# Seven-product output projection: order of the weight loads, order of the second pair's splits, and where two more chunks get their offset

## The chip, the cores and the metric

The kernel runs on one core of a Trainium2 chip. The metric is the device time of one execution in microseconds (us), lower is better. A run of the kernel before was timed three times: 1286.32, 1286.92 and 1287.92 us.

## What is computed

One layer of a bidirectional encoder for 2048 rows of 1024 columns, float32 throughout. A joint input projection feeds a chunked gated linear attention (4 heads) and a latent attention with a softmax (4 heads). Each gives 512 columns. They are joined, go through one output projection, and the residual and a LayerNorm close the layer. The change lies in this last part alone:

```python
def hybrid_mixer(...):
    ...
    return jnp.concatenate([o_a, o_b], axis=-1) @ w_out       # (2048 x 1024) @ (1024 x 1024)

x = layer_norm(DEEPNORM_ALPHA * x + mixed, ln_g, ln_b)        # alpha = 2 ** 0.25
```

## The kernel before, in words

**Products.** TensorE multiplies in a type with a shorter mantissa, so each float32 operand is split into a rounded part (`hi`, line 393, a copy on ScalarE) and a remainder (`lo`, line 400, here a subtraction on GpSimd). `mm3` (line 448) runs three matmuls for one product, so lines 450 to 452 are most of TensorE's work.

**Chunks and pairs.** The output projection works on 16 chunks of 128 rows. Chunks 0 to 7 are multiplied in the plain way: 8 slices of the inner dimension, two halves of 512 columns. They run partly under the last block of the attention, chunks 4 and 5 right behind it, and chunks 6 and 7 at places 0 to 21.76. Chunks 8 to 15 make four pairs (class `Pair`, line 1969). A pair's 256 rows and the 1024 inner columns form 2 x 2 blocks A11, A12 (row 0 of the pair) and A21, A22 (row 1). Instead of eight block products it has seven, P1 to P7, with sums of the blocks (S1 = A21 + A22, S3, S2 = S1 - A11, S4 = A11 - A12, computed in place by `add` on VectorE, line 2016) and with sums of weight blocks. P5, P6 and P7 use the weight combinations wt1, wt2, wt3. P4 uses wt4, which is loaded over the right half (columns 512 on) of the weight tiles 0 to 3, once chunk 7 has read them. The combinations were computed early in the kernel and lie in DRAM as high and low parts: `fetch_t("2l")` loads the low part of wt2, and so on. wt1, wt2 and wt3 have 1 MB a part; the low part of wt3 goes in two loads of 512 KB, into tiles `wt3l` and `wt3m`; wt4 takes eight loads of 256 KB (`fetch_t("4h")`, `"4l"`, line 2213).

**Loads of a pair.** `Pair.load(r)` (lines 1982 to 1995) issues four DMAs of 256 KB for row r of the pair: the first half's data, two gate factors, the second half's data. The gate factors are multiplied in on GpSimd (`gate`, line 2004). The second pair's row 0 goes into a tile that the profile calls `lng`, its row 1 into `lnb`; these are the former tiles of the LayerNorm's scale and offset. All these DMAs are issued by SyncE (SP), in one queue.

**Banks.** The seven products of a pair share four PSUM banks. P1 and P7 use bank 0, P5 and P2 bank 1, P6 bank 2, P3 and P4 bank 3. So P4 may begin when VectorE has read P3 (`R6`), the next pair's P1 when ScalarE has copied P7 (`c7`, line 2041), and its P5 when VectorE has read P2 (`R7`). `read` is lines 2051 and 2053, `sum` line 2044, and the statistics are line 2059.

**Closing a chunk.** `finish_a` subtracts the mean and multiplies by ln_g on VectorE (line 2315; `centre`, line 2084, for row 0). ScalarE makes the reciprocal root (lines 2321 to 2326). `finish_b` multiplies by it and adds ln_b on VectorE (line 2332), once for each half, and issues the stores. Only the last pair's row 0 is closed by ScalarE (scale, line 2094) and GpSimd (offset, line 2095), from a copy of ln_b made by `copy_lnb` (line 2088).

**Order.** Every engine runs its instructions in the order in which they stand. From chunk 6 on, the order is a sort by hand-written places (`put`, and `PLACE_PAIR`, lines 135 to 152); a place is meant as microseconds. Pair p starts at T = 21.76 + 19.05 p. An entry of the second pair with place -9.85 thus stands among the first pair's entries at 9.2. Before chunk 6, the order on ScalarE, GpSimd and SP is that of the code in lines 1907 to 1936.

Of the kernel before, what the change touches and what calls it, by code (L numbers as in the profile page):

```python
# [136 lines left out]
    load1=(-23.6, -35.9),  # L137
    res=(-10.0, -8.0),
    gate=((-19.94, -18.58), (-24.72, -21.3)),
    add=dict(S1=-10.55, S3=-9.85, S2=-8.0, S4=-4.37),  # L140
    hi=dict(A11=-17.26, S1=-9.75, S2=-7.3, A12=-5.39, S3=-4.77, S4=-3.53, A22=-2.66),
    lo=dict(A11=-13.14, S1=-8.45, S2=-6.6, S3=-3.67, A22=1.77, A12=3.13, S4=4.49),
    product=dict(P1=0.0, P5=2.72, P6=5.44, P3=8.16, P7=10.88, P2=13.6, P4=16.32),
    last=dict(P1=0.0, P5=2.72, P6=5.44, P3=8.16, P2=10.88, P7=13.6, P4=16.32),
    gate1=((-14.6, -13.3), (-19.95, -18.6)),
    gate0=((-6.0, -4.7), (-24.72, -21.3)),
    first=dict(hA11=-15.2, hS3=-8.0, hA12=-2.6, lS3=-6.5, lS4=-2.2),
    read=dict(c1=2.78, R1=5.9, R5=6.5, R5b=7.1, U2=9.9, R2=10.5, R6=11.87, c7=14.91, U3=15.63, R3=16.26, bn22=16.89,
              R7=17.52, sq=18.25, R4=20.34, R4b=20.97, bn21=21.6, rs=21.9, fa=(22.9, 22.23), fb=(23.9, 26.7)),
    read_last=dict(c1=2.78, lnb=9.0, R1=3.3, R5=6.3, R5b=6.9, U2=8.9, R2=9.5, R3=10.1, R4b=10.7, R6=11.5, bn12=12.1,  # L150
                   R7=14.1, bn11=14.7, R3p=16.9, R4p=17.5, bn22=18.1, fa=(15.3, 20.2), fb=(17.0, 20.3)),
)

# [232 lines left out]
class K:  # L386
# [1215 lines left out]
    def attention(self):  # L1602
# [4 lines left out]
        with ExitStack() as ctx:  # L1607
# [245 lines left out]
            for k in range(NK):  # L1853
                if k < PRE_W:
                    v = NP * (PRE_BLOCK + k)
                    hi, lo = v + out["pre_hi"], v + out["pre_lo"]
                else:
                    hi = end + out["w_hi"] + (k - PRE_W) * out["w_step"]
                    lo = hi + out["w_lo"]
                if k == 0:  # L1860
                    put(hi - 6, op.fetch_w, k)
                put(hi, op.split_hi, k)
                put(lo, op.split_lo, k)
                if k + 1 < NK:
                    put(lo + 0.01, op.fetch_w, k + 1)
                else:
                    put(max(lo, end + 26) + 0.02, op.load_ln)
                for o, place in zip(first, out["part0"]):
                    put(end + (out["part"][k] if k else place), op.part, o, k)
            for c, o in enumerate(first):  # L1870
# [98 lines left out]
class Pair:  # L1969
# [117 lines left out]
        self.lnb = self.op.bp.tile([P, 2, 512], F32, tag="pl", name="lnbc", bufs=3)  # L2087
        self.nc.scalar.activation(self.lnb, self.op.ln[1], AF.Copy)

    def finish_first(self):  # L2090
        o, c = self.rows[0], self.c[0]
        for n in range(2):
            rr = o["rr"][:, n]
            self.nc.scalar.activation(rr, rr, AF.Copy, scale=o["rs"])
            self.nc.gpsimd.tensor_tensor(rr, rr, self.lnb[:, n], ALU.add)
            self.nc.sync.dma_start(self.k.out[c * P:(c + 1) * P, n * 512:(n + 1) * 512], rr)

    def put(self, put, T, last):
        at = lambda place, fn, *a: put(T + place, fn, *a)
        P_, op = PLACE_PAIR, self.op  # L2100
        first = {} if self.p else P_["first"]
        if self.p:
            for r in (1, 0):
                at(P_["load1" if self.p == 1 else "load"][r], self.load, r)
# [40 lines left out]
        at(e["bn11"], self.stats, 0, 0, 0)  # L2145
        at(e["bn22"], self.stats, 1, 1, 2, 3)
# [6 lines left out]
        at(e["fb"][0], self.finish_first)  # L2153
        at(e["fa"][1], op.finish_a, self.rows[1])
        at(e["fb"][1], op.finish_b, self.rows[1])

# [1 line left out]
class OutProj:  # L2158
# [47 lines left out]
    def fetch_t(self, n):  # L2206


        j, p = int(n[0]), "hl".index(n[1])
        src, kern = self.k.wt_s[j][p], self.k  # L2210
        if j == 4:
            for k in range(4):
                self.nc.sync.dma_start(self.W[k][p][:, 512:].bitcast(F32), src[:, k])
            return
        if n == "3l":
            t = [kern.wof.tile([P, D], F32R, tag="raw", name="wt3l", bufs=1).rearrange("p (a d) -> p a d", a=2),
                 kern.keep.tile([P, 2, QB], F32R, tag="acc", name="wt3m")]
            for i in range(2):
                self.nc.sync.dma_start(t[i].bitcast(F32), src[:, 2 * i:2 * i + 2])
        else:  # L2220
            slot = dict(zip(("1h", "1l", "2h", "2l", "3h"), ("ckvT_h", "ckvT_l", "krs", "vh", "vl")))[n]
            t = kern.rp.tile([P, NKT, P], F32R, tag=f"res_{slot}", name=f"wt{n}").rearrange("p (k a) d -> p k (a d)", k=4)
            self.nc.sync.dma_start(t.bitcast(F32), src)
            t = [t[:, 0:2], t[:, 2:4]]
        self.T[j, p] = t

    def wt(self, j, k):
        return [self.T[j, p][k // 2][:, k % 2] for p in range(2)]
# [64 lines left out]
    def residual(self, o, n):  # L2293
# [6 lines left out]
        nc.vector.bn_stats(o["bn"][:, n], rr)  # L2300

    def finish(self, o):
        self.finish_a(o)
# [98 lines left out]
```

## Time and profile before

| what | value |
|---|---|
| runs shown, median (range) | 1286.92 us (1286.32 to 1287.92) |
| profiled execution, its own time | 1286.29 us |
| its span, first to last instruction | 1284.5 us |
| TensorE busy | 1257.6 us, 98% of the span |
| VectorE / ScalarE / GpSimd busy | 941.5 / 874.0 / 846.9 us |
| mean granted TensorE clock | 0.996 of full speed |

The profile is one execution. Times in its views are microseconds from the span's start; 1.8 us of the execution lie around the span. PE is TensorE, PEld its weight loads, DVE VectorE, ACT ScalarE, POOL GpSimd, SP (or SPq) SyncE, which issues the DMAs. A timeline row has the start, the duration, the engine, the source line, the operation, what is written and read, a count, and in brackets the idle time ahead of it with what ended it. `pw` are the four banks of the pairs, `xr` the rows of a chunk of a pair, `of`, `lng` and `lnb` loaded data of a pair, `A11h` and `A11l` the two parts of a block.

### The profile page before, as it was taken

What the parts mean: (1) busy time and instruction counts of PE and PEld (TensorE: products, weight loads), DVE (VectorE), ACT (ScalarE), POOL (GpSimd) and SP (SyncE); (2) the same over time, 40 slices, a digit from 0 to 9 for tenths busy, and PEclk for the clock granted to TensorE, in tenths of its full rate; (3) what the DMA queues carried; (4) which work ended last, traced back from release to release, by engine and by line L of the source; (5) the groups of instructions that cost most, each with busy time, mean ns of one, the idle gap of its engine ahead of it and who ended that gap; (6) DMA issues with size and microseconds to landing.
All of it is one profiled execution on the core that took longest, in us unless ns stands there. A gap on an engine that the chain in (4) does not pass through costs nothing.

```text
span 1284.5 us, 20176 instructions
## 1 busy us (share of the span) xinstructions
PE 1257.6 (98%) x6928; PEld 1110.4 (86%) x6928; DVE 941.5 (73%) x1706; ACT 874.0 (68%) x1549; POOL 846.9 (66%) x546
## 2 busy tenths in 40 slices
PE   7999999999999999999999999999999999999997
PEld 7999999999889999999788888888888888888785
DVE  6865775656675455555798888888888888658788
ACT  7765657666675656665688888888888888614454
POOL 0244555363667666672188888889999999955762
PEclk9999999999999999999999999999999999999998
DMA  9332525353675565565501111122123211469952
GB/s 298 97 93 63 173 74 170 89 155 101 197 243 166 183 220 182 180 207 163 164 1 41 42 42 41 42 58 59 57 58 92 68 55 34 170 188 309 356 183 80
DMA packets 122518, 166.81 MB, mean 130 GB/s; under 512 B 18502, under 2 KB 71118, under 8 KB 121776
## 3 DMA queue, kind: packets, MB, share of 16 engines
q1 hardware_dynamic: 114256, 163.39, 40.2%
q0 software_dynamic: 768, 2.10, 0.5%
q8 instruction: 55, 0.90, 0.4%
q10 hardware_dynamic: 7392, 0.03, 0.3%
q14 instruction: 47, 0.39, 0.2%
HBM read 106.72 MB, written 58.75 MB: 129 GB/s over the span
## 4 chain that ended last, share of the span: by engine, by line
PE 56%; POOL 4%; issue 3%; DMA 3%; DVE 3%; ACT 3%; SPq 0%; DVEq 0%; POOLq 0%; ACTq 0%
PE pS L1636 4%; PE o L452 4%; PE o L450 4%; PE o L451 4%; PE pS L1637 4%; PE pS L1638 4%; PE pS L1639 4%; PE pS L1640 4%; PE pz L451 2%; PE pz L452 2%; PE pz L450 2%; PE ipm L452 1%; PE ipm L450 1%; PE ipm L451 1%; PE po L451 1%
## 5 line engine op out<-in xcount | busy, mean ns | idle before, releaser
L402 POOL TENSOR_TENSOR pl<-s,ph 128x1024 fp32r<-128x1024 f32 x128 | 306.1, 2416 | 56.6 <-ACT ph L396 56.6
L1658 DVE TENSOR_TENSOR rm<-pS,rm 128x512 f32<-128x512 f32 x210 | 144.8, 689 | 26.5 <-ACT s L1645 20.9
L1682 DVE TENSOR_TENSOR s<-s,mb 128x1024 f32<-128x1024 f32 x128 | 151.2, 1213 | 9.4 <-PE mb L1676 9.3
L1645 ACT ACTIVATE s<-pS 128x1024 f32<-128x1024 f32 x128 | 131.4, 1027 | 37.7 <-PE pS L1640 33.5
L396 ACT ACTIVATE ph<-s 128x1024 fp32r<-128x1024 f32 x128 | 134.9, 1057 | 13.5 <-PE o L452 12.9
L1686 ACT ACTIVATE s<-s 128x1024 f32<-128x1024 f32 x128 | 131.5, 1051 | 13.4 <-DVE s L1682 13.3
L450 PE MATMUL ipa<-wah,xah 128*128 128x384 f32 (+1 forms) x384 | 130.2, 339 | 6.1 <-ACT wah L396 6.0
L1099 POOL TENSOR_TENSOR Us<-Us,cw 128x512 f32<-128x512 f32 x16 | 18.6, 1163 | 174.2 <-DVE Us L1097 158.7
L451 PE MATMUL ipa<-wal,xah 128*128 128x384 f32 (+1 forms) x384 | 125.1, 326 | 0.2 <-DVE wal L402 0.2
L452 PE MATMUL ipa<-wah,xal 128*128 128x384 f32 (+1 forms) x384 | 125.2, 326 | 0.0
L1636 PE MATMUL pS<-qh,ckvT_h 128*128 128x512 f32 x256 | 102.6, 401 | 0.8 <-DVE rm L1658 0.4
L450 PE MATMUL o<-ph,vh 128*128 128x512 f32 x256 | 101.1, 395 | 0.0
L1637 PE MATMUL pS<-ql,ckvT_h 128*128 128x512 f32 x256 | 99.9, 390 | 0.0
L1638 PE MATMUL pS<-qh,ckvT_l 128*128 128x512 f32 x256 | 99.9, 390 | 0.0
L1639 PE MATMUL pS<-rh,krs 128*128 128x512 f32 x256 | 99.8, 390 | 0.0
L1640 PE MATMUL pS<-rl,krs 128*128 128x512 f32 x256 | 99.8, 390 | 0.0
L452 PE MATMUL o<-ph,vl 128*128 128x512 f32 x256 | 99.8, 390 | 0.0
L451 PE MATMUL o<-pl,vh 128*128 128x512 f32 x256 | 99.7, 389 | 0.0
L1709 DVE TENSOR_TENSOR ap<-ap,s 128x512 f32<-128x512 f32 x120 | 83.1, 692 | 3.5 <-ACT ap L1701 0.7
L450 PEld LDWEIGHTS ipa<-wah,xah 128*128 128x128 f32 x384 | 73.4, 191 | 6.9 <-ACT wah L396 6.3
L450 PE MATMUL pz<-xch,wzh 128*128 128x256 f32 x256 | 74.8, 292 | 0.0
L451 PEld LDWEIGHTS ipa<-wal,xah 128*128 128x128 f32 x384 | 73.4, 191 | 1.2 <-DVE wal L402 0.6
(446 smaller groups left out, 3897.7 us busy)
## 6 DMA issues: line engine op xcount, KB each, us to landing
xcf<-xT_dram SPq DMA_DIRECT2D x16, 512.0 KB, 4.6
xr<-x_dram SPq DMA_DIRECT2D x16, 512.0 KB, 6.3
xaf<-xT_dram SPq DMA_DIRECT2D x14, 512.0 KB, 3.7
wb<-wO_dram SPq DMA_DIRECT2D x16, 256.0 KB, 3.5
oib<-oi_s SPq DMA_DIRECT2D x16, 256.0 KB, 4.3
qdb<-qd_s SPq DMA_DIRECT2D x16, 256.0 KB, 5.1
SU<-su_s SPq DMA_DIRECT2D x16, 256.0 KB, 4.5
ub<-u_s SPq DMA_DIRECT2D x16, 256.0 KB, 4.7
```

Source lines behind the costliest of these rows:

```text
L396: return nc.scalar.activation(dst, src, AF.Copy).ins
L402: return e.tensor_tensor(dst, src, hi.bitcast(F32), ALU.subtract).ins
L450: mm(out, ah, bh, start=start, stop=False)
L451: mm(out, ah, bl, start=False, stop=False)
L452: mm(out, al, bh, start=False, stop=stop)
L1636: mm(ps[:, e], kh, qh, start=True, stop=False)
L1637: mm(ps[:, e], kh, ql, start=False, stop=False)
L1638: mm(ps[:, e], kl, qh, start=False, stop=False)
L1639: mm(ps[:, e], kr, rh, start=False, stop=False)
L1640: mm(ps[:, e], kr, rl, start=False, stop=True)
L1658: V.tensor_tensor(d["rm"], src[:, e], d["rm"], ALU.max)
L1682: V.tensor_tensor(s, s, d["mb"][:, None, :].to_broadcast([P, 2, QB]), ALU.subtract)
```

## The change

Four things are changed.

- **Weight loads.** The low part of wt2 and the high part of wt3 are issued directly behind the load of chunk 5, where they stood behind the load of chunk 7 and chunk 5's residual rows. The first half of wt3's low part (`3l`) is issued behind the loads of ln_g and ln_b, during the last attention block; the second half (`3m`) stays at place 1.0. The eight loads of wt4 go from place 21.9 to 16.4. The load of row 0 of the second pair stands at 17.21, before and after.
- **The second pair.** Its A11 is split at T - 10 and T - 9, where it was T - 17.26 and T - 13.14. Its S3 goes from T - 9.85 to T - 8.2, its S2 from T - 8.0 to T - 7.5. For the later pairs S2 goes to T - 7.6. `R6` goes from 11.87 to 11.3. So `R6` stands ahead of the next pair's S2 on VectorE, where it stood behind it.
- **Offset on GpSimd.** The third pair's two chunks are closed as the last pair's row 0 is: ScalarE scales, GpSimd adds ln_b. The copy of ln_b is made at T - 1.5 of the last pair, where it was T + 9.
- **A small order.** The last block's `rcp` on VectorE is ordered behind chunk 4's last statistics.

```diff
@@ PLACE_PAIR
-    add=dict(S1=-10.55, S3=-9.85, S2=-8.0, S4=-4.37),
-    hi=dict(A11=-17.26, S1=-9.75, S2=-7.3, A12=-5.39, S3=-4.77, S4=-3.53, A22=-2.66),
-    lo=dict(A11=-13.14, S1=-8.45, S2=-6.6, S3=-3.67, A22=1.77, A12=3.13, S4=4.49),
+    add=dict(S1=-10.55, S3=-9.85, S2=-7.6, S4=-4.37),
+    hi=dict(A11=-17.26, S1=-9.75, S2=-7.0, A12=-5.39, S3=-4.77, S4=-3.53, A22=-2.66),
+    lo=dict(A11=-13.14, S1=-8.45, S2=-6.5, S3=-3.67, A22=1.77, A12=3.13, S4=4.49),
...
+    second=dict(hA11=-10.0, lA11=-9.0, aS3=-8.2, hS3=-5.3, aS2=-7.5),
...
-    read=dict(c1=2.78, R1=5.9, R5=6.5, R5b=7.1, U2=9.9, R2=10.5, R6=11.87, c7=14.91, U3=15.63, R3=16.26, bn22=16.89,
-              R7=17.52, sq=18.25, R4=20.34, R4b=20.97, bn21=21.6, rs=21.9, fa=(22.9, 22.23), fb=(23.9, 26.7)),
-    read_last=dict(c1=2.78, lnb=9.0, R1=3.3, ...
+    read=dict(c1=2.78, R1=5.9, R5=6.5, R5b=7.1, U2=9.9, R2=10.5, R6=11.3, c7=14.91, U3=15.63, R3=16.26, bn22=16.89,
+              R7=17.52, sq=18.25, R4=20.34, R4b=20.97, bn21=21.6, rs=21.9, fa=(22.9, 22.23), fb=(23.9, 26.7), late=(24.2, 24.8)),
+    lnb=-1.5,
+    read_last=dict(c1=2.78, R1=3.3, ...
@@ attention
                     put(max(lo, end + 26) + 0.02, op.load_ln)
+                    put(max(lo, end + 26) + 0.03, op.fetch_t, "3l")
...
                 load(5)
+                op.fetch_t("2l")
+                op.fetch_t("3h")
                 split(4)
                 load(6)
...
                 load(7)
                 op.load_res(rest[5])
-                op.fetch_t("2l")
-                op.fetch_t("3h")
...
-                        rcp(nb - 1)
+                        with self.after(rest[4]["last"]):
+                            rcp(nb - 1)
...
-            put(1.0, op.fetch_t, "3l")
-            put(21.9, op.fetch_t, "4h")
-            put(21.91, op.fetch_t, "4l")
+            put(1.0, op.fetch_t, "3m")
+            put(16.4, op.fetch_t, "4h")
+            put(16.41, op.fetch_t, "4l")
+            op.last_pair = pairs[-1]
@@ class Pair
-    def finish_first(self):
-        o, c = self.rows[0], self.c[0]
+    def finish_off(self, o):
+        c = o["c"]
         for n in range(2):
             rr = o["rr"][:, n]
             self.nc.scalar.activation(rr, rr, AF.Copy, scale=o["rs"])
...
-        first = {} if self.p else P_["first"]
+        first = P_[("first", "second")[self.p]] if self.p < 2 else {}
...
-                at(P_["add"][n], self.add, n)
+                at(first.get(f"a{n}", P_["add"][n]), self.add, n)
...
             for r in range(2):
-                at(e["fb"][r], op.finish_b, self.rows[r])
+                if op.last_pair.p == self.p + 1:
+                    at(e["late"][r], op.last_pair.finish_off, self.rows[r])
+                else:
+                    at(e["fb"][r], op.finish_b, self.rows[r])
             return
-        at(e["lnb"], self.copy_lnb)
+        at(P_["lnb"], self.copy_lnb)
```

`fetch_t` is rewritten so that `"3l"` and `"3m"` are separate calls; its DMAs are the same. `residual` keeps the statistics instruction as `o["last"]` for the small order.

More of the change, by code (lines that the diff above doesn't have):

```diff
@@ L146 @@
     gate0=((-6.0, -4.7), (-24.72, -21.3)),
+    second=dict(hA11=-10.0, lA11=-9.0, aS3=-8.2, hS3=-5.3, aS2=-7.5),
     first=dict(hA11=-15.2, hS3=-8.0, hA12=-2.6, lS3=-6.5, lS4=-2.2),
-    read=dict(c1=2.78, R1=5.9, R5=6.5, R5b=7.1, U2=9.9, R2=10.5, R6=11.87, c7=14.91, U3=15.63, R3=16.26, bn22=16.89,
-              R7=17.52, sq=18.25, R4=20.34, R4b=20.97, bn21=21.6, rs=21.9, fa=(22.9, 22.23), fb=(23.9, 26.7)),
-    read_last=dict(c1=2.78, lnb=9.0, R1=3.3, R5=6.3, R5b=6.9, U2=8.9, R2=9.5, R3=10.1, R4b=10.7, R6=11.5, bn12=12.1,
+    read=dict(c1=2.78, R1=5.9, R5=6.5, R5b=7.1, U2=9.9, R2=10.5, R6=11.3, c7=14.91, U3=15.63, R3=16.26, bn22=16.89,
+              R7=17.52, sq=18.25, R4=20.34, R4b=20.97, bn21=21.6, rs=21.9, fa=(22.9, 22.23), fb=(23.9, 26.7), late=(24.2, 24.8)),
+    lnb=-1.5,
+    read_last=dict(c1=2.78, R1=3.3, R5=6.3, R5b=6.9, U2=8.9, R2=9.5, R3=10.1, R4b=10.7, R6=11.5, bn12=12.1,
                    R7=14.1, bn11=14.7, R3p=16.9, R4p=17.5, bn22=18.1, fa=(15.3, 20.2), fb=(17.0, 20.3)),
@@ L2152, in put @@
         at(e["fa"][0], op.finish_a, self.rows[0])
-        at(e["fb"][0], self.finish_first)
+        at(e["fb"][0], self.finish_off, self.rows[0])
         at(e["fa"][1], op.finish_a, self.rows[1])
@@ L2206, in fetch_t @@
     def fetch_t(self, n):
-        j, p = int(n[0]), "hl".index(n[1])
-        src, kern = self.k.wt_s[j][p], self.k
+        kern, sync = self.k, self.nc.sync
+        j = int(n[0])
         if j == 4:
+            p = "hl".index(n[1])
             for k in range(4):
-                self.nc.sync.dma_start(self.W[k][p][:, 512:].bitcast(F32), src[:, k])
+                sync.dma_start(self.W[k][p][:, 512:].bitcast(F32), kern.wt_s[j][p][:, k])
             return
[L2215 to L2225, printed above, removed]
+        if n in ("3l", "3m"):
+            i = "lm".index(n[1])
+            if i:
+                t = kern.keep.tile([P, 2, QB], F32R, tag="acc", name="wt3m")
+            else:
+                t = kern.wof.tile([P, D], F32R, tag="raw", name="wt3l", bufs=1).rearrange("p (a d) -> p a d", a=2)
+            sync.dma_start(t.bitcast(F32), kern.wt_s[j][1][:, 2 * i:2 * i + 2])
+            self.T[j, 1] = self.T.get((j, 1), []) + [t]
+            return
+        p = "hl".index(n[1])
+        slot = dict(zip(("1h", "1l", "2h", "2l", "3h"), ("ckvT_h", "ckvT_l", "krs", "vh", "vl")))[n]
+        t = kern.rp.tile([P, NKT, P], F32R, tag=f"res_{slot}", name=f"wt{n}").rearrange("p (k a) d -> p k (a d)", k=4)
+        sync.dma_start(t.bitcast(F32), kern.wt_s[j][p])
+        self.T[j, p] = [t[:, 0:2], t[:, 2:4]]
     def wt(self, j, k):
@@ L2299, in residual @@
         nc.vector.scalar_tensor_tensor(rr, o["xr"][:, n], ALPHA, o["ps"][n], ALU.mult, ALU.add)
-        nc.vector.bn_stats(o["bn"][:, n], rr)
+        o["last"] = nc.vector.bn_stats(o["bn"][:, n], rr).ins
     def finish(self, o):
```

## The prediction

> **What bounds the kernel now.** The page says that TensorE is busy for 98% of the span, so I looked first for its idle time, in the waits of TensorE. Everything before chunk 6 can be left aside; the change touches only what follows and some loads. From 1190 us on one wait is left:
>
> ```profile
> PE pw L450 <- DVE xr L2053: 1.9, 1, 1.9
> ```
>
> The timeline of TensorE shows where it is, and what else was lost:
>
> ```profile
> 1210.24 0.39 PE L452 MATMUL pw<-woh,A12l 128*128 128x512 f32 x1
> ...
> 1212.57 0.55 PE L450 MATMUL pw<-woh,A22h 128*128 128x512 f32 x1 [1.94 <-DVE xr L2053]
> ...
> 1217.01 0.40 PE L450 MATMUL pw<-woh,A11h 128*128 128x512 f32 x1
> ...
> 1258.13 0.50 PE L450 MATMUL pw<-wt1h,S1h 128*128 128x512 f32 x1
> ...
> 1274.62 0.28 PE L452 MATMUL pw<-woh,A22l 128*128 128x256 f32 x1
> ```
>
> P4 of the first pair waits for `R6`, and its 12 matmuls take 4.44 us, where 12 x 0.227 are 2.72 (the 180 matmuls from 1217.01 to 1258.13 take 41.12 us, 0.228 each with two small losses). In the stretches of time the granted clock there is half. So this place costs TensorE 2.1 + 1.7 = 3.8 us. The same view tells how full the DMA engines are:
>
> ```profile
> 1184.00:1188.00 4.00, 4.00 (x19) 3.32 (x18) 3.90 (x7) 1.27 (x2) 2.03 (x2) 1.00 0.82 253
> 1206.00:1210.00 4.00, 4.00 (x19) 3.31 (x18) 1.66 (x3) 0.30 (x1) 3.92 (x3) 1.00 1.05 397
> 1213.00:1216.00 3.00, 3.00 (x9) 2.32 (x8) 1.99 (x3) 2.25 (x5) 1.49 (x2) 0.50 1.09 309
> ```
>
> But is TensorE what ends last? Its last matmul ends at 1274.90, and VectorE reads that result only at 1277.10. VectorE is 2.2 us behind. From 1190 us on its waits name everybody but TensorE:
>
> ```profile
> DVE of L2016 <- POOL of L2004: 4.8, 1, 4.8
> DVE xr L2332 <- ACT ln_r L2326: 2.7, 3, 1.1
> DVE lng L2016 <- POOL S2l L402: 2.9, 2, 1.5
> DVE lng L2016 <- POOL A11l L402: 2.5, 1, 2.5
> DVE of L2016 <- POOL S2l L402: 1.5, 1, 1.5
> DVE rr L2332 <- ACT ln_r L2326: 0.4, 1, 0.4
> ```
>
> and its timeline shows an even beat:
>
> ```profile
> 1210.17 1.74 DVE L2016 TENSOR_TENSOR lng<-s,lng 128x512 f32<-128x512 f32 x1 [2.47 <-POOL A11l L402]
> ...
> 1213.97 0.69 DVE L2016 TENSOR_TENSOR lng<-lng 128x512 f32<-128x512 f32 x1 [1.46 <-POOL S2l L402]
> ...
> 1216.64 0.67 DVE L2053 TENSOR_TENSOR xr<-pw,xr 128x512 f32<-128x512 f32 x1
> ...
> 1230.53 0.68 DVE L2016 TENSOR_TENSOR of<-s,of 128x512 f32<-128x512 f32 x1
> 1231.13 0.69 DVE L2053 TENSOR_TENSOR xr<-pw,xr 128x512 f32<-128x512 f32 x1
> 1233.29 1.76 DVE L2016 TENSOR_TENSOR of<-of 128x512 f32<-128x512 f32 x1 [1.48 <-POOL S2l L402]
> ...
> 1237.03 0.68 DVE L2053 TENSOR_TENSOR xr<-pw,xr 128x512 f32<-128x512 f32 x1
> ...
> 1277.10 0.41 DVE L2053 TENSOR_TENSOR xr<-pw,xr 128x256 f32<-128x256 f32 x1
> ```
>
> `R7` comes at 1216.64 and 1237.03: 20.39 us a pair, where TensorE needs 84 x 0.227 = 19.04. So the bound from the second pair on is **VectorE's chain**, and it begins at 1210.17, when S2 of the second pair may overwrite A11. That hangs on GpSimd and on a DMA:
>
> ```profile
> 1205.80 3.08 POOL L2004 TENSOR_TENSOR lng<-lng,gr 128x512 f32<-128x512 f32 x2 [1.65 <-DMA lng<-ob_s]
> 1208.84 1.29 POOL L402 TENSOR_TENSOR A11l<-lng,A11h 128x512 fp32r<-128x512 f32 x1
> ...
> 1233.21 1.29 POOL L2004 TENSOR_TENSOR lnb<-lnb,gr 128x512 f32<-128x512 f32 x1
> ```
>
> The 3.8 us of TensorE are hidden behind this chain: even at the last pair, P5 starts at 1258.13 only 0.1 us late.
>
> **The change part by part.**
>
> *wt4 ahead of the second pair's row 0.* On SP the order now is:
>
> ```profile
> 1142.96 1.84 SPq L2244 DMA_DIRECT2D of<-ob_s  x1
> 1149.92 0.32 SPq L2241 DMA_DIRECT2D of<-oa_s  x1
> ...
> 1161.86 0.43 SPq L2223 DMA_DIRECT2D wt2l<-wt2l_s  x1
> ...
> 1180.69 0.33 SPq L1992 DMA_DIRECT2D of<-oa_s  x1
> ...
> 1198.21 0.53 SPq L1995 DMA_DIRECT2D lng<-ob_s  x1
> 1198.83 2.93 SPq L2213 DMA_DIRECT2D woh<-wt4h_s  x4
> 1201.93 3.78 SPq L2213 DMA_DIRECT2D wol<-wt4l_s  x4
> ```
>
> At 16.4 the eight loads pass the four of row 0 (17.21). The engines are full (1.05 of their share), so row 0 lands later by what wt4 takes: 2.10 MB at 397 GB/s, the rate while wt4 was moving, are 5.3 us. `3l`, 0.52 MB, no longer stands ahead: -1.3. At 1184 to 1188 the engines had 0.7 us of room, into which an emptier queue moves up; I take -0.5. That gives +3.5 for the landing. It could be nothing, if wt2's and wt3's earlier departure empties the queue, and at most 5.3. The two gate multiplications took 3.08 us beside VectorE's S1 and S3; alone they take 2 x 1.29, -0.5. So A11l ends **+3.0** later, at 1213.1. Behind the waiting gates GpSimd has A11l, the low parts of S1 and S2, and the third pair's gates; VectorE has S2, S4 and the reads of P6, P7 and P2. Nothing hides this: S2 stood waiting already.
>
> The Trainium skill, in "DMA: Bandwidth & Descriptors", section "Specifications", gives a limit of about 358 GB/s from HBM for one core. By it wt4 would take 5.9 us and the landing come 0.4 us later still; the trace does not agree, as its row has 397.
>
> *R6 ahead of S2.* In the first pair's window P4 no longer waits: `R6` now stands behind S3, which needs row 0's first part; that is issued and lands ahead of the second part, on which A11l hangs. TensorE's 3.8 us are regained, but the next wait takes them. `c7` stands on ScalarE behind the splits of S2 and A12:
>
> ```profile
> 1213.52 0.58 ACT L2041 ACTIVATE pc<-pw 128x512 f32<-128x512 f32 x1
> ...
> 1258.11 1.06 ACT L2069 ACTIVATE xr<-xr 128x1024 f32<-128x1024 f32 x1 [1.50 <-DVE xr L2053]
> ```
>
> It ended 3.97 us behind A11l (1214.10 against 1210.13), so it will end at 1217.1, and P1 of the second pair overwrites what it reads. P1 starts at about 1217.1, where it started at 1217.01. What P4 gains, P1 gives back.
>
> In the second and third windows S2 moves behind `R6`, 1231.13 in place of 1230.53: 0.6 us. S2's splits, S4 and all behind it follow, as VectorE stands idle for S2l there. Two windows: **+1.2**. At least nothing, at most 2 x 0.7.
>
> *S4 in the first window.* It took 0.69 us at 1213.97, when GpSimd was waiting for a DMA, and 1.76 at 1233.29, when GpSimd had begun a multiplication 0.08 us before. In the new order the third pair's data has landed by then (nothing added stands ahead of it), so GpSimd goes on at once behind S2l: **+1.1**, between nothing and 1.1.
>
> *Two more chunks on GpSimd.* These three groups are from 1255 to 1285:
>
> ```profile
> L2332 DVE SCALAR_TENSOR_TENSOR xr<-xr,ln_r,ln 128x512 f32<-128x512 f32 x6 | 4.2, 743 | 0.5 <-ACT ln_r L2326 0.4
> L2095 POOL TENSOR_TENSOR xr<-xr,lnbc 128x512 f32<-128x512 f32 x2 | 2.5, 1266 | 15.3 <-ACT xr L2094 15.3
> L2094 ACT ACTIVATE xr<-xr,ln_r 128x512 f32<-128x512 f32 x2 | 1.3, 716 | 0.0
> ```
>
> VectorE loses four operations of 0.70, 2.8 us, in the last window, ahead of everything that ends last. TensorE's last result allows 2.2 of these; its earlier results, P2 and P7, hold VectorE up by some 0.2. **-2.0**, between -1.4 and -2.2. GpSimd gets 4 x 1.25 us in its idle 15.3, ScalarE 4 x 0.67 behind the third pair's roots, with nothing due there until the last pair's. The stores wait for GpSimd on SP, with only the last pair's stores behind them. The copy of ln_b (1.0 us) moves into ScalarE's idle 1.50 ahead of 1258.11. If that cover were gone, the squares would be 1 us late.
>
> *The early loads.* wt2l and wt3h go into the 5.1 us between 1144.80 and 1149.92 in which SP waits for a buffer; `3l` into SP's wait for chunk 0's rows. Issuing costs nothing. Their 2.1 MB delay chunk 6's load and the first stores by up to 5.3 us. Chunk 3's residual reuses a stored buffer, and through the roots and splits the load at 1180.69 could move by as much. I take nothing; up to 1.5 us more on row 0's landing is in the range. The order of `rcp` costs nothing, as no later instruction is moved past it.
>
> *Sum.* 3.0 + 1.2 + 1.1 - 2.0 = **+3.3 us**. The profiled execution took 1286.29, so 1289.6; the median of the runs shown is 0.6 above it, so **1290.2**.
>
> **The rivals.**
>
> *Row 0 lands no later.* The earlier loads leave the queue so empty that wt4 is through in time. Then A11l ends 0.5 earlier, and -0.5 + 1.2 + 1.1 - 2.0 = -0.2: 1286.7. Against it: from 1206 to 1210 the engines are full, and 5.3 us of work pass in front. For it: 2.6 MB leave the stretch. Without S4's and S2's delays it is 1284.4.
>
> *The stall is what counts.* TensorE, not VectorE, sets the end, and the change does what it says: -3.8 - 2.0, 1281.1. This is decided by A11l: `R7` ends 7.2 us behind it, and P5 of the second pair would be due at 1210.46 + 2 x 2.72 = 1215.9, so A11l must end by 1208.7, 1.4 us earlier than now. For it: TensorE's 98%. Against it: VectorE's waits.
>
> *The clock falls in the last pair.* With VectorE's beat at 20.39 + 0.6 = 21.0, TensorE waits 1.9 us a pair, ahead of P5. The row at 1213 shows half the clock behind a wait of 1.94. In the last pair that takes 1.7 us away from the -2.0: 1291.9. Against it: with a slow stretch in the third pair the last wait is short. The Trainium skill, in "TensorE: Matmul & The Clock Gate", section "HAM oscillation — how this bites in real kernels", names gaps above about 3.4 us as the danger; by that rule nothing would be lost here, and the trace does not agree, as 1.94 was enough.
>
> **How the numbers follow.** The forecast gets 0.42, with a range of its own from 1288.7 to 1291.7; row 0 no later 0.30; the clock 0.15; the stall 0.13. A measurement of this kernel can tell about 0.2%, 2.6 us, from no change: 1284.3 to 1289.5. Of the forecast I put 0.31 above that and 0.11 within; of row 0 no later 0.28 within and 0.02 below; the clock is above, the stall below. Faster 0.15, same 0.39, slower 0.46. The range leaves out the stall and little more: 1284.2 to 1292.8.
>
> **What would show it.** Right: `lng<-ob_s` issued behind wt4, the gates of `lng` starting near 1209; P4 of the first pair without a wait, but P1 or P5 of the second with one on ScalarE or VectorE; `R7` at a beat near 21.0; VectorE's last read within 0.3 us of the last matmul. Wrong: the gates of `lng` before 1206, or no wait on TensorE behind 1200 and an end set by its last matmul.

## The result, and the profile after

The kernel after takes 1292.74 us in the median of five runs (1292.36 to 1293.55), the kernel before 1287.34 (1286.32 to 1288.43): a ratio of 1.0043, with a 95% interval from 1.0028 to 1.0057. So the change costs 5.4 us, with an interval of 3.6 to 7.3. The forecast was +3.3, just below it. Single executions of e1, e3 and e4, below, took 3101 to 5409 us; the ratios leave them out, and e3's only profile is one of them. The profiled execution of after is the slowest of its five: 1293.55 us, span 1291.8. In after's listing the lines have moved: `lo` is line 404, `mm3` 452 to 454, `add` 2021, the copies c1 and c7 2046, `read` 2056 and 2058, `gate` 2009, `Pair.load` 1997 to 2000, `fetch_t` 2222 to 2236.

Waits of TensorE, then of VectorE, from 1190 us on:

```profile
PE pw L452 <- ACT pc L2046: 4.8, 1, 4.8
PE pw L452 <- DVE xr L2058: 1.8, 2, 1.3
```

```profile
DVE lng L2021 <- POOL A11l L404: 5.5, 1, 5.5
DVE lng L2021 <- POOL S2l L404: 4.1, 2, 2.1
DVE of L2021 <- POOL S2l L404: 2.1, 1, 2.1
DVE xr L2058 <- PE pw L454: 0.7, 1, 0.7
```

The wait ahead of P4 is gone. In its place P1 of the second pair waits 4.8 us for `c7`, and VectorE waits 5.5 us for A11l, where it waited 2.5. New is the last row: VectorE now waits for TensorE. The timeline of TensorE shows P4 starting without a wait, P1 and a P5 with one, and the last matmul:

```profile
1212.98 0.39 PE L452 MATMUL pw<-woh,A22h 128*128 128x512 f32 x1
...
1220.67 0.79 PE L452 MATMUL pw<-woh,A11h 128*128 128x512 f32 x1 [4.81 <-ACT pc L2046]
...
1267.29 0.50 PE L452 MATMUL pw<-wt1h,S1h 128*128 128x512 f32 x1 [1.28 <-DVE xr L2058]
...
1283.82 0.28 PE L454 MATMUL pw<-woh,A22l 128*128 128x256 f32 x1
```

SP's timeline of after, from chunk 3's load over the early loads to row 0 of the second pair:

```profile
1115.99 0.43 SPq L2253 DMA_DIRECT2D of<-oa_s  x1
...
1124.19 0.33 SPq L2230 DMA_DIRECT2D wt3l<-wt3l_s  x1
...
1145.65 0.62 SPq L2236 DMA_DIRECT2D wt2l<-wt2l_s  x1
1146.37 1.69 SPq L2236 DMA_DIRECT2D wt3h<-wt3h_s  x1
...
1197.25 2.09 SPq L2222 DMA_DIRECT2D woh<-wt4h_s  x4
1199.87 3.14 SPq L2222 DMA_DIRECT2D wol<-wt4l_s  x4
1203.07 0.42 SPq L1997 DMA_DIRECT2D lng<-oa_s  x1
```

and of before, one row for the start of the comparison:

```profile
1115.37 0.42 SPq L2241 DMA_DIRECT2D of<-oa_s  x1
```

Chunk 3's load, the first row of after and the row of before, comes ahead of anything that the change moves; after is already 0.62 us late there. The profiles of this case have such offsets against before of -0.8 (f3) to +1.8 us (e1), and they have to be taken off before two profiles are compared.

What hangs on row 0 is in GpSimd's and VectorE's timelines:

```profile
1212.78 2.65 POOL L2009 TENSOR_TENSOR lng<-lng,gr 128x512 f32<-128x512 f32 x2 [6.55 <-DMA lng<-ob_s]
1215.39 1.27 POOL L404 TENSOR_TENSOR A11l<-lng,A11h 128x512 fp32r<-128x512 f32 x1
```

```profile
1216.70 1.73 DVE L2021 TENSOR_TENSOR lng<-s,lng 128x512 f32<-128x512 f32 x1 [5.50 <-POOL A11l L404]
1220.48 1.74 DVE L2021 TENSOR_TENSOR lng<-lng 128x512 f32<-128x512 f32 x1 [2.04 <-POOL S2l L404]
...
1224.20 0.67 DVE L2058 TENSOR_TENSOR xr<-pw,xr 128x512 f32<-128x512 f32 x1
...
1245.38 0.67 DVE L2058 TENSOR_TENSOR xr<-pw,xr 128x512 f32<-128x512 f32 x1
...
1266.56 0.67 DVE L2058 TENSOR_TENSOR xr<-pw,xr 128x512 f32<-128x512 f32 x1
...
1284.28 0.41 DVE L2058 TENSOR_TENSOR xr<-pw,xr 128x256 f32<-128x256 f32 x1
```

Of before, one more row is needed, its last `R7`:

```profile
1257.41 0.67 DVE L2053 TENSOR_TENSOR xr<-pw,xr 128x512 f32<-128x512 f32 x1
```

Read against the rows of before, the chain adds up: A11l ends 6.53 us later (1216.66 against 1210.13); from there to `R7` it takes 1.03 more; the beat, from `R7` to `R7`, is 21.18 in place of 20.39, 0.8 more in each of two windows; from the last `R7` to VectorE's last read it takes 17.72 in place of 19.69, 1.97 less. Sum +7.2, the difference of the two spans (7.3).

### The profile page after: what moved, and what is told of

Same layout as the page of the kernel before. It is cut to its first block, busy times and chain, and to the rows that moved or that the text cites. A ratio compares the mean times of both kernels' runs of the same rounds, so it can differ in the third digit from the quotient of the medians.

```text
span 1291.8 us, 20181 instructions
## 1 busy us (share of the span) xinstructions
PE 1260.0 (98%) x6928; PEld 1110.9 (86%) x6928; DVE 939.5 (73%) x1702; ACT 876.2 (68%) x1553; POOL 851.5 (66%) x550
## 4 chain that ended last, share of the span: by engine, by line
PE 79%; DVE 5%; POOL 3%; DMA 3%; ACT 3%; issue 2%; SPq 0%; DVEq 0%; POOLq 0%; ACTq 0%
PE o L454 4%; PE o L452 4%; PE pS L1638 4%; PE o L453 4%; PE pS L1639 4%; PE pS L1640 4%; PE pS L1641 4%; PE pS L1642 4%; PE ipa L452 4%; PE ipa L454 4%; PE ipa L453 3%; PE pz L453 2%; PE pz L454 2%; PE pz L452 2%; PE ipg L452 2%
```

## The experiments

The theory, A below: VectorE's chain sets the end, and it begins with the landing of the second pair's row 0. The rivals: B, the early loads cost the time; C, TensorE's stalls set the end; D, the early loads make room in the queue; E, VectorE's work or its port sets the beat; F, each wait that is taken away only shows the next. Every kernel was timed against the kernel before on the same chip; that median lay between 1286.35 and 1287.46.

### e1_wt4_behind: wt4 alone put back

```diff
-            put(16.4, op.fetch_t, "4h")
-            put(16.41, op.fetch_t, "4l")
+            put(21.9, op.fetch_t, "4h")
+            put(21.91, op.fetch_t, "4l")
```

> The kernel after, with wt4's eight loads back behind the second pair's row 0. Theory A (row 0's landing sets VectorE's chain): in the profile of after wt4 takes 1202.51 to 1209.18 = 6.7 us at the queue just ahead of row 0. Without it the gates of lng start 5.7 to 6.7 us earlier, near 1206.6, A11l ends near 1210.4, and as the third pair's row then lands behind wt4, S4 of the first window loses its 1.05 us too. 1292.7 - 6.2 - 1.05 = 1285.5 us. Theory B (the early loads alone cost the time, through the chunks' buffers): the gates of lng still start after 1210, 1292 us. Theory C (TensorE's stalls set the end): P4's stall is gone already, so no stall changes, 1292.7.

Measured: 1286.72 us, ratio 1.0003 (0.9994 to 1.0012). The whole loss is gone with this one edit: it is worth 1.0043 - 1.0003 = 0.4%, 5.1 us. B and C, as they were put, fall. A is confirmed in the place; its total was 1.2 us too low.

### e4_wt4_alone: the kernel before, wt4 alone moved

The same two lines in the other direction.

> The kernel before, with wt4's loads alone moved to place 16.4, ahead of the second pair's row 0. Theory A: the landing of lng is 5.7 to 6.7 us later, S2, R6 and P4 with it, and S4 of the first window takes 1.05 us more as the third pair's data lands before it: 1287.3 + 6.2 + 1.05 = 1294.5 us, with TensorE's stall ahead of P4 grown from 1.9 to some 8 us. Theory B: 1287.3, as no early load is moved. Theory D (the queue has room for wt4 where it now stands): 1287.

Measured: 1295.4 us, ratio 1.0067 (1.0054 to 1.0080): the move alone costs more than the whole change. The size is A's, the path only partly. ScalarE's timeline:

```profile
1210.34 0.63 ACT L396 ACTIVATE A11h<-lng 128x512 fp32r<-128x512 f32 x1 [6.62 <-DMA lng<-oa_s]
1210.87 0.58 ACT L2041 ACTIVATE pc<-pw 128x512 f32<-128x512 f32 x1
```

The split of A11 stands ahead of the first pair's `c1` and waits 6.6 us for row 0, so `R1` and TensorE's P7 wait too. The change's new place for that split (T - 10) takes this away. That would explain why the move of wt4 costs 8.5 us alone and 5.1 inside the change; the split's place was not tried by itself.

### e2_early_undone: after, without the early loads

```diff
                 load(5)
-                op.fetch_t("2l")
-                op.fetch_t("3h")
...
                 op.load_res(rest[5])
+                op.fetch_t("2l")
+                op.fetch_t("3h")
...
-                    put(max(lo, end + 26) + 0.03, op.fetch_t, "3l")
...
+            put(0.99, op.fetch_t, "3l")
```

> The kernel after, with the three early loads back at their old places (wt2l and wt3h behind chunk 5's residual rows, the first half of wt3's low part just ahead of the second), wt4 still ahead of row 0. Theory A: chunk 3's residual goes back by 2.6 us, row 0 of the first pair is issued near 1180.7, and the queue ahead of wt4 is 2.5 earlier but has 1.3 us of wt3's low part more in it: the landing of lng is 1.3 us earlier, 1291.4 us. Theory B (early loads cost everything): 1287.3. Theory D (the early loads emptied the queue, as they were meant to): without them 2.6 MB come back ahead of wt4, the landing is up to 5 us later, 1296.

Measured: 1292.36 us, ratio 1.0041 (1.0029 to 1.0053), the same as after. B and D fall. A's 1.3 us lie inside the interval, and so does nothing at all. The profile does not settle it either: its gates of `lng`

```profile
1212.15 2.66 POOL L2009 TENSOR_TENSOR lng<-lng,gr 128x512 f32<-128x512 f32 x2 [6.29 <-DMA lng<-ob_s]
```

start, with its offset of 1.05 us off, 1.1 us ahead of after's; but those of e4, which has no early loads either, start when after's do.

### e3_early_alone and g3_early_again: the early loads alone

The kernel before with the diff's three early loads and its `fetch_t`, timed twice; the profile is the second one's.

> The kernel before, with the three early loads alone. Theory A: as in the profile of after, chunk 3's residual waits for the store that the 2.1 MB delay, 2.5 us on the chunks' chain, less the 1.3 us of the first half of wt3's low part that no longer stands ahead of row 0: the landing of lng is 1.2 to 1.3 later than before, 1288.6 us. Theory B (early loads cost everything): 1292. The forecast on record took nothing for them: 1287.3. Theory D (they empty the queue): 1286.8 or less.

> The kernel before, with the three early loads alone, once more. The forecast on record took nothing for them: 1286.9. Theory A with the profile of after: chunk 3's residual waits 1.7 us, row 0 of the first pair is issued up to 2.6 us later, the queue ahead of the second pair's row 0 is 1.3 us later in the end, 1288.2.

Measured: 1287.54 us, ratio 1.0003 (0.9994 to 1.0012), and 1287.53, ratio 1.0010 (1.0001 to 1.0019). So +0.4 and +1.2 us. The second run's profile shows how; SP, VectorE and GpSimd:

```profile
1116.55 0.44 SPq L2246 DMA_DIRECT2D of<-oa_s  x1
...
1183.93 0.33 SPq L1993 DMA_DIRECT2D of<-oa_s  x1
...
1197.89 0.33 SPq L1993 DMA_DIRECT2D lng<-oa_s  x1
```

```profile
1163.19 1.28 DVE L2304 SCALAR_TENSOR_TENSOR rr<-xr,po 128x512 f32<-128x512 f32 x2 [0.80 <-DMA of<-oa_s]
```

```profile
1207.76 3.11 POOL L2005 TENSOR_TENSOR lng<-lng,gr 128x512 f32<-128x512 f32 x2 [1.17 <-DMA lng<-ob_s]
```

The same residual in before, VectorE:

```profile
1160.20 1.28 DVE L2299 SCALAR_TENSOR_TENSOR rr<-xr,po 128x512 f32<-128x512 f32 x2
```

With the offset of 1.18 us (1116.55 against 1115.37) taken off, the residual is 1.8 us later than before, row 0 of the first pair is issued 2.1 later, `lng` is issued 0.7 later, and its gates start 0.8 later. But before is an early profile: it has to be held against all eleven usable profiles without any early load (before, e2, e4, e5, e6, e9, f1, f2, f3, g1, h1) and all three with the change's three (g3, e1, after), each with its offset off (the five kernels that move `3l` and row 0 are left aside):

| place | without, us | with, us |
|---|---|---|
| start of chunk 3's residual | 1160.2 to 1161.6 | 1162.0 to 1162.3 |
| issue of the first pair's row 0 | 1180.7 to 1182.1 | 1182.6 to 1182.8 |
| issue that follows the residual rows and stores (`lng` or wt4) | 1196.0 to 1197.3 | 1196.6 to 1196.9 |

So the chunks do come later, by some 1.4 us in the mean at row 0, and the last row shows that this eats what `3l` gives back: the issue there is neither earlier nor clearly later. What held the residual is not settled: the profile names a load that it does not read.

### e5_offset_alone: the offset on GpSimd alone

The diff's `finish_off`, `late` and `lnb` on the kernel before.

> The kernel before, with the third pair's two chunks closed by ScalarE and GpSimd, alone. Theory A (VectorE's chain sets the end, TensorE is 2.2 us ahead of it): four operations of 0.70 us leave VectorE in the last window, TensorE's last result holds it up from then on, 2.0 us less, 1284.9 where the kernel before takes 1286.9. Theory C (TensorE sets the end): nothing, 1286.9. Theory E (GpSimd's adds of 1.25 us, beside VectorE, lock its additions and the gain goes into them): 1286 to 1287.

Measured: 1285.01 us, ratio 0.9981 (0.9970 to 0.9991), 2.1 us less than before. The row that the forecast asked for is in VectorE's waits, which in before name TensorE nowhere:

```profile
DVE xr L2055 <- PE pw L453: 0.8, 1, 0.8
```

### e6_order_alone: the new order alone

The diff's `second`, `R6`, and the places of S2, on the kernel before.

> The kernel before, with the new places of R6, S2, S3 and of the second pair's splits, alone; wt4, the early loads and the offset as before. Theory A: in the profiles of after and of the kernel with wt4 behind row 0, VectorE's beat is 21.18 us where before has 20.39, in two windows: +1.6; the gates of lng run 0.4 us faster without S1 and S3 beside them: 1286.9 + 1.6 - 0.4 = 1288.1 us, P4's wait gone from TensorE, a wait ahead of P1 or P5 of the second pair in its place. Theory C (TensorE's stall of 3.8 us at P4 sets the end): 1283.1.

Measured: 1288.93 us, ratio 1.0016 (1.0007 to 1.0024), 1.9 us more. C wanted 3.8 less and falls. Measured alone, the order (+1.9), the early loads (+0.4 and +1.2) and the offset (-2.1) add up to about nothing, as e1 found them together. Where P4's gain went is in TensorE's timeline:

```profile
1214.28 0.50 PE L451 MATMUL pw<-woh,A11h 128*128 128x512 f32 x1 [0.65 <-ACT pc L2042]
...
1217.50 0.50 PE L451 MATMUL pw<-wt1h,S1h 128*128 128x512 f32 x1 [0.21 <-DVE xr L2054]
...
1226.20 0.80 PE L453 MATMUL pw<-woh,S4l 128*128 128x512 f32 x1 [2.49 <-POOL S4l L403]
```

P1 and P5 give back 0.9 us; the rest goes at P3 of the second pair, which waits for the low part of S4 on GpSimd. No forecast had named that one.

### e9_s2_earlier: S2 moved the other way

```diff
-    add=dict(S1=-10.55, S3=-9.85, S2=-8.0, S4=-4.37),
+    add=dict(S1=-10.55, S3=-9.85, S2=-9.3, S4=-4.37),
```

The first two pairs keep -8.0.

> The kernel before, with S2 of the third and fourth pair moved the other way, ahead of U2 and R2 on VectorE (place T - 9.3 in place of T - 8.0); nothing else. Theory A: U2, R2 and R6 then fill the time in which VectorE waits 1.46 to 1.48 us for the low part of S2, so its beat falls from 20.39 by up to 1.3 us to TensorE's 19.05; the end moves by what VectorE is behind TensorE, 2.2 us, and no more: 1286.9 - 2.0 = 1284.9 us. Theory C (TensorE sets the end already): 1286.9. Theory E (the beat is VectorE's work, not its wait): 1286.9, with the wait moved to another place.

Measured: 1286.27 us, ratio 0.9996 (0.9987 to 1.0005). E holds. VectorE's timeline, S2, S4 and `R7` of one window and `R7` of the next:

```profile
1230.76 1.75 DVE L2016 TENSOR_TENSOR of<-s,of 128x512 f32<-128x512 f32 x1
...
1234.59 1.76 DVE L2016 TENSOR_TENSOR of<-of 128x512 f32<-128x512 f32 x1
...
1238.33 0.67 DVE L2053 TENSOR_TENSOR xr<-pw,xr 128x512 f32<-128x512 f32 x1
...
1258.63 0.67 DVE L2053 TENSOR_TENSOR xr<-pw,xr 128x512 f32<-128x512 f32 x1
```

S4 waits no more, but S2 now runs beside GpSimd's low part of S1 and takes 1.75 us in place of 0.68. The wait became a locked port; the beat is 20.30.

### f1 to f4: S2 in a tile of its own

S4 is the difference of A12 and S2, and S2 lies where A11 lay (the description of the kernel above says A11 - A12, which is wrong). So S4 must wait until GpSimd has made the low part of S2. If S2 is written over S1, whose low part is finished by then, nothing waits. In these four kernels S4 is computed as A12 - A11, with the same instruction and size; from g1 on it is A12 - S2 again.

```diff
-                            S2=lambda: (a11, self.s1, a11, ALU.subtract), ...
+                            S2=lambda: (self.s1, self.s1, a11, ALU.subtract), ...
```

> The kernel before, with S2 written over S1's tile in place of A11's, so that S4 no longer waits for the low part of S2; S4 of the third and fourth pair stands right behind S2, and in the second pair the low part of S1 comes ahead of that of A11. R6 stays behind S2, the offset on VectorE. Theory A (VectorE's chain): its wait of 1.46 to 1.48 us a window goes, and S4 starts while GpSimd stands idle, so it takes 0.69 us in place of 1.76. The beat falls from 20.39 us to TensorE's 19.05 or near it; the end moves by what VectorE is behind TensorE at the end, 2.2 us: 1287.1 - 2.0 = 1285.1 us, and P4's wait stays. Theory C (TensorE sets the end): 1287.1. Theory E (VectorE's work sets the beat, as when S2 was moved ahead of U2, where the beat came out at 20.30): 1286.3.

Measured: 1285.46 us, ratio 0.9989 (0.9980 to 0.9997), 1.4 us less than before. Two rows of VectorE, `R7` of the second and third pair, give a beat of 19.0:

```profile
1234.88 0.67 DVE L2054 TENSOR_TENSOR xr<-pw,xr 128x512 f32<-128x512 f32 x1
...
1253.90 0.68 DVE L2054 TENSOR_TENSOR xr<-pw,xr 128x512 f32<-128x512 f32 x1
```

f2 makes this of f1:

```diff
-    second=dict(aS4=-4.37, lS1=-9.7, lA11=-9.6),
+    second=dict(aS2=-7.1, aS4=-7.0, lS1=-9.7, lA11=-9.6),
```

With it goes e5's offset.

> The kernel before this one, with R6 ahead of S2 in the second pair alone, and the third pair's offset on GpSimd. Theory A: with the chain shorter by 2 us a window, what P4 gains (its wait of 1.9 us and the 1.7 us of halved clock behind it) is no longer given back at P1 and P5, and the offset takes VectorE off the end: 1287.1 - 3.6 - 2.0 = 1281.5 us, a beat of 19.1 and no wait over 0.5 us on TensorE behind P3 of the first pair. If the first window's chain (row 0 lands as before) still gives half of it back: 1283.

Measured: 1287.01 us, ratio 1.0003 (0.9993 to 1.0013), 5.5 us over A. Here theory A fell as it stood; TensorE's waits and a stretch of time (PE's time, its busy time, clock, share of the DMA engines, GB/s) say why:

```profile
PE pw L454 <- POOL S4l L404: 3.9, 1, 3.9
```

```profile
1226.00:1232.00 6.00, 6.00 (x21) 0.72 0.95 261
```

P3 of the second pair waits 3.9 us for the low part of S4, which stands on GpSimd behind four gates of the third pair and three other low parts; a granted clock of 0.72 in the mean of the six microseconds from 1226 on follows. P4's gain moved there whole. GpSimd's order belongs to the chain.

> The kernel before this one, with the gates of the first pair's row 0 ahead of the low part of its S2 on GpSimd, where they stood behind that of S3. Several profiles show P3 of the first pair waiting for the low part of S4, 0.3 to 2.5 us, which hangs on these gates; VectorE waits 4.8 us for them. Theory A: this wait goes, and nothing else: 0 to 1 us less than the kernel before this one, 1281. If P6 of the first pair then waits for the low part of S2, which is 0.9 us later: no change.

> The kernel before this one, with the loads of the second pair's row 0 ahead of the first pair's residual rows, and the first half of wt3's low part during the last attention block. Theory A (the landing of row 0 starts VectorE's chain): the gates of lng start up to 3.9 us earlier; if the chain of the first window was still what the end hung on, up to 1 us less, if TensorE is the bound by then, no change: 1280 to 1281. Against it: the residual rows land 2.6 us later, and R1 of the first pair could wait for them.

Measured: 1286.82 us, ratio 1.0000 (0.9992 to 1.0009), and 1286.03, ratio 0.9995 (0.9985 to 1.0004). f3's reason was a misreading: the wait for S4l is P3's of the second pair, not of the first. Both kernels still have that wait, of 4.4 and 3.9 us.

### g1_s4_low_first and i1_all_in_order: that wait taken away

```diff
-    second=dict(aS2=-7.1, aS4=-7.0, lS1=-9.7, lA11=-9.6),
+    second=dict(aS2=-7.1, aS4=-7.0, lS1=-9.7, lA11=-9.6, lS4=-2.2),
```

> The kernel with S2 in its own tile, R6 ahead of S2 in the second pair, and the third pair's offset on GpSimd, with the low part of the second pair's S4 ahead of the third pair's last gates on GpSimd (place T - 2.2 in place of T + 4.49). Theory A (VectorE's and GpSimd's chain held TensorE up, and TensorE is the bound when it does not): P3's wait of 3.85 us and the 1.3 us of lower clock behind it go, no wait over 0.5 us is left on TensorE behind the first pair, its last matmul ends 3.8 us or more ahead of before's, 1286.9 - 3.8 - 2.0 = 1281.1 us. Theory F (each wait that is taken away shows the next one): a wait of 1 us or more stands elsewhere on TensorE, 1284 or more.

Measured: 1283.62 us, ratio 0.9980 (0.9969 to 0.9990), 2.7 us less than before. F: TensorE keeps a wait of 2.2 us. It is that of P4 of the second pair, for `R6`, which in this window stands behind the third pair's S2 and S4: the first window's stall, one pair later (the expectations of h1 and i1 name P5, wrongly). i1 is the same with f4's loads and gates, so it differs from f4 in the low part of S4 and S4's operand alone:

```diff
-    load1=(-23.6, -35.9),
+    load1=(-27.2, -35.9),
-    gate0=((-6.0, -4.7), (-24.72, -21.3)),
+    gate0=((-8.3, -8.2), (-24.72, -21.3)),
+    first=dict(res=(-8.1, -7.9), ...
```

`res` are the first pair's residual rows; `3l` is loaded where after loads it.

> The kernel with S2 in its own tile, R6 ahead of S2 in the second pair, the third pair's offset on GpSimd and the second pair's low part of S4 early, with the gates of the first pair's row 0 ahead of the low part of its S2 on GpSimd, row 0 of the second pair loaded behind these gates and ahead of the first pair's residual rows, and the first half of wt3's low part loaded during the last attention block. Theory A: row 0's landing and the first pair's gates no longer hold the chain, no wait over 0.5 us is left on TensorE behind the first pair, and P5's 2.2 us come back: 1283.6 - 2.2 = 1281.4 us where the kernel before takes 1286.5. Against it: R1 of the first pair waits 1.8 us for its residual rows, which VectorE's chain takes: 1282.5. Theory F (something else bounds the end): 1283.6.

Measured: 1281.56 us (1280.94 to 1283.76), ratio 0.9954 (0.9940 to 0.9967): **5.9 us faster than before**, and by the two ratios some 11 us faster than after. TensorE's waits from 1190 on, and the gates of `lng` on GpSimd:

```profile
PE pw L452 <- DVE xr L2057: 1.3, 1, 1.3
```

```profile
1202.67 2.67 POOL L2008 TENSOR_TENSOR lng<-lng,gr 128x512 f32<-128x512 f32 x2
```

The gates wait for nothing and start 3.1 us earlier than before's, TensorE keeps 1.3 us of that same wait, where A wanted none over 0.5, and VectorE waits 2.2 us for the first pair's residual rows, as the forecast against A had it. Its profiled execution is one of its slower ones (1283.23), so two profiles show only 3.1 of the 5.9 us; the interval rests on the runs.

### e8, g2, h1 and h2: loads that stand ahead of the gates

In these four the loads of a later row's factors stand ahead of gates that still need the tile, so the gates multiply by the later row's factors and wait for them: in e8_all_lifted and g2_row0_ahead the first pair's row 0 (g2 lacked the earlier gates that its expectation names), in h1_s1_low_first and h2_all_ordered the second pair's.

> The kernel before, with R6 ahead of S2 in the first pair's window alone, S2 of the later pairs ahead of U2 and R2, the third pair's offset on GpSimd, the first half of wt3's low part early, row 0 of the second pair loaded ahead of the first pair's residual rows, and the first pair's gates of row 0 ahead of the low part of its S2 on GpSimd; wt4 where it was. Theory A: the landing of lng comes up to 3.9 us earlier (2.6 for the residual rows, 1.3 for wt3's half), A11l ends near 1206.5, R6 and S2 come without a wait, P4's 3.8 us are regained and the beat lets TensorE keep them: the last matmul near 1271.1 in place of 1274.9, 1286.9 - 3.8 - 2.0 = 1281.1 us. Theory D (the loads that row 0 passes are late in its place: the residual rows hold up R1): 1284 or more. If VectorE's chain is not lifted by the earlier row 0: 1285, by the offset alone.

> The same, with the gates of the first pair's row 0 earlier on GpSimd, row 0 of the second pair loaded ahead of the first pair's residual rows, and the first half of wt3's low part loaded during the last attention block. Theory A: with TensorE as the bound the earlier landing brings nothing, 1281; if the first window's chain still holds TensorE, up to 1 us less. Against it: R1 of the first pair then waits for its residual rows, 1.8 us in the run before, which VectorE's chain has to take: 1282.

> The kernel with S2 in its own tile, R6 ahead of S2 in the second pair, the third pair's offset on GpSimd and the second pair's low part of S4 early, with the low part of the second pair's S1 ahead of the gates of lng on GpSimd. Theory A: S2 of the second pair no longer waits 1.7 us, S4 then waits for the gates instead; R7 of the first pair comes about 1.0 us earlier, and P5's wait of 2.2 us falls to 1.2: 1283.6 - 1.0 = 1282.6 us. Theory F (something else bounds the end): no change, 1283.6.

> The same, with the gates of the first pair's row 0 ahead of the low part of its S2 on GpSimd, row 0 of the second pair loaded behind these gates and ahead of the first pair's residual rows, and the first half of wt3's low part loaded during the last attention block. Theory A: the landing of row 0 comes 2 to 4 us earlier, the gates of lng no longer hold S4, and no wait over 0.5 us is left on TensorE behind the first pair: 1283.6 - 2.2 = 1281.4 us. Against it: R1 of the first pair waits for its residual rows, which VectorE's chain takes: 1282.5. Theory F: 1283.6.

Measured: 1293.03 us, ratio 1.0051 (1.0035 to 1.0067); 1285.39, 0.9992 (0.9983 to 1.0001); 1292.08, 1.0043 (1.0029 to 1.0057); 1291.44, 1.0035 (1.0022 to 1.0048). None tells what it was made for. h1 tells something else: it is g1 with the gates of `lng` held up by a DMA, on GpSimd

```profile
1217.66 2.60 POOL L2007 TENSOR_TENSOR lng<-lng,gr 128x512 f32<-128x512 f32 x2 [9.59 <-DMA gr<-gm_s]
```

and by the two ratios it loses 0.6%, 8.1 us, against g1, with a wait of 12.1 us for A11l on VectorE that g1 does not have: theory A once more, without any move of wt4.

## Why the forecast was right in its places and wrong in its size

- **What bounds the kernel: right.** A single edit on the landing of row 0 carries the loss (e1), and taking away P4's stall alone gains nothing (e6).
- **wt4's passage: right.** 5.3 us were forecast for its passing. Counted from the issue that stands behind the residual rows and stores in both kernels (1196.03 for `lng` before, 1197.25 for wt4 after) to the gates of `lng`, before takes 9.77 us and after 15.53: 5.8 us. The same stretch takes 14.4 and 14.9 us in e2 and e4, and 9.6 to 11.2 in the ten profiles with wt4 behind row 0 and the gates' loads as in before (before, e1, e5, e6, e9, f1, f2, f3, g1, g3). So single profiles leave the passage anywhere from 3 to 6 us; the means differ by 4.9. They do not tell the 397 GB/s that I took from the Trainium skill's figure of 358 GB/s ("DMA: Bandwidth & Descriptors", section "Specifications"), by which the estimate was 5.9.
- **The early loads: the step that failed.** "Issuing costs nothing ... I take nothing", beside two credits: -1.3 for `3l`, -0.5 for room. These 1.8 us of credit did not come. With the early loads the issue ahead of which wt4 stands comes at 1196.6 to 1196.9, without them at 1196.0 to 1197.3 (the table at g3). The runs agree: alone the early loads cost 0.4 and 1.2 us, where a credit of 1.8 would have given a ratio of 0.9986, outside both intervals; and without them after's 1.0043 would have become 1.0057, outside e2's. The prediction had named the path (chunk 3's residual, the roots, the splits, the load at 1180.69), and then put it in the range instead of the sum. Without the credits the sum is +5.1, where +5.4 was measured.
- **A11l in all:** +3.0 forecast, +6.5 measured in the two profiles: 1.8 are the credits that did not come, 0.5 wt4, 0.6 the offset between two executions, and 0.6 no more than before's place at the early end of the table. The gates without S1 and S3 beside them gained the 0.5 forecast, or nearly (2.65 us for 3.08).
- **S4 in the first window: right.** 1.74 us for 0.69; the stretch from A11l to `R7` is 1.03 longer, +1.1 forecast.
- **S2 behind R6: right, a little low.** 0.8 us a window for 0.6: in before `R6` filled 0.6 of the time in which S4 waits for S2l; now that wait is 2.07 in place of 1.48. Alone the order costs 1.9 us (e6), as P3's wait comes with it.
- **P1 gives back what P4 gains: right.** `c7` was 4.8 us late. No end hangs on it, as TensorE waits again behind it, for `R7` ahead of two P5s (1.8 us in two waits).
- **Two chunks on GpSimd: right.** -2.0 forecast, -1.97 in the profiles, -2.1 alone (e5).
- **What would show it.** The gates were to start near 1209; they started at 1212.78. The beat was to be 21.0, it is 21.18. VectorE's last read was to come within 0.3 us of the last matmul: 1284.28, and the last matmul ends at 1284.10.
- **The rivals.** Row 0 no later: no. The stall: no, but not for good, since i1 gets some of it once the chain is short. The clock in the last pair: no; the wait ahead of P5 is 1.28 us and the clock stays full, so the time beyond the forecast is not that rival's.

Open: the profiled executions differ by 7.3 us, the medians by 5.4, as after's profiled execution is 0.8 above its median and before's 1.1 below. 0.6 of that is the offset seen at 1115 us; what makes it was not tried. How the delay gets from chunk 3's residual to the load of row 0 was read from profiles and not tried alone. What the last waits in g1 and i1 cost was not settled either: h1 and h2 were to tell it and could not.

## What to carry to other kernels

A stall on the busiest engine is worth its length only if no other engine's chain ends as late: look for the last wait of the engine that reads the last result, and follow it back to its first cause, here a DMA. Here a load moved ahead in a full queue cost about what it moves at the rate of that stretch, and the loads moved away gave nothing back, as they delayed what fills the same queue later; look for what the earlier place now holds up. One profile of each kernel is not enough for differences below some 1.5 us, not even at a common landmark: hold them against the spread of the kernels that the edit does not touch. After each wait that goes, look for the next in the order of *every* engine of the chain: here ScalarE's copy, VectorE's sum and GpSimd's low part came one after the other. Single steps gained up to 2.7 us against before (g1); with all three moved and the loads in order it was 5.9 (i1).

## What was not expected of the hardware

**The clock.** In after the granted clock is half from 1220 to 1226, behind the wait of 4.81 us. Two waits of the same length ended differently. TensorE's stretches behind the wait of 2.49 us in e6, then behind one of 2.48 us in e1:

```profile
1226.00:1229.00 3.00, 2.80 (x7) 0.50 0.96 286
```

```profile
1229.00:1232.00 3.00, 2.79 (x12) 1.00 0.84 265
```

Behind the waits of 1.28 us in after and 1.3 us in i1 the clock stayed full; 1.94 cost it in before. In all profiles but e3's, from 1196 us to the last matmul, no wait of up to 1.76 us lowered the clock (f1 has that one) and every one from 3.27 us did (e5); in between, the waits of 1.88 (e8), 1.94, 2.15 (g1), 2.17 (g3) and 2.49 us did, those of 2.02 and 2.05 (both e9) and 2.48 us did not. So the length alone does not decide here between 1.9 and 2.5 us, and the rule of the Trainium skill ("TensorE: Matmul & The Clock Gate", section "HAM oscillation — how this bites in real kernels") that gaps above about 3.4 us are the dangerous ones is too mild for this kernel.

**The port.** An addition of two SBUF tiles on VectorE takes 0.68 us, and 1.73 to 1.76 in the rows shown here, where a subtraction or multiplication on GpSimd had started just before. The Trainium skill ("SBUF — State Buffer", section "SBUF: two separate sides") calls the shared port an exclusive lock; the trace agrees, with a price of 1.07 us, and e9 shows that moving an operation away from a wait can move it into the lock.

**The queue.** In before, SP's four issues of wt4's low part wait 0.2, 0.2, 0.5 and 0.7 us, each for the landing of the load eight issues ahead of it (`lng<-oa_s`, the two gate factors, `lng<-ob_s`). In this stretch the landings pace the issues.
